# A Relu that writes back to its PSUM bank, in the index scores of a hybrid encoder trunk

## The chip, the cores and the metric

The kernel runs on one core of a Trainium2 chip. The time is the device time of one execution in microseconds (us); a kernel's number is the median of its runs. One further execution was recorded by the hardware profiler; all rows shown are of that one.

## What is computed

Two layers of a trunk over 512 frames of width 1024. Each layer projects the normalised input, runs four groups of mixers, gates them and adds the output projection:

```python
for l in range(DEPTH):
    h = _rmsnorm(x, norm_g[l])
    p = _split(h @ w_in[l])
    o_a = _mla(...)          # latent attention
    o_b = _diff_attn(...)    # differential attention, two maps per head
    o_c = _dsa(p["c_q"], p["c_k"], p["c_v"], p["c_qidx"], p["c_kidx"], p["c_widx"], rel_bias, topk)
    o_d = _short_conv(...)
    x = x + concat(o_a * silu(a_gate), ..., o_d * silu(d_gate)) @ w_out[l]
return _rmsnorm(x, final_g)
```

The change lies in group C, sparse attention, where an indexer of 8 heads scores every key for every query and each query attends to its 128 best keys:

```python
score = relu(einsum('bqhd,bkd->bqhk', qi, kidx))
index = einsum('bqh,bqhk->bqk', wi, score) * idx_scale
index = where(_chunk_mask(qpos, kpos)[None], index, NEG)
_, sel = lax.top_k(index, topk)
```

## The kernel before

Queries are worked in four blocks of 128 (`qb`), keys up to the end of the query's block, so a tile has `W = (qb + 1) * 128` columns. Large products are made as three float32r matmuls of high and low parts (`mm3`, L128); the parts are split by ScalarE (L107, L116, L119) and by GpSimd (L102) or VectorE (L117, L120).

A layer is a sequence of slots. Each slot merges streams of work: a `pair` of attention units (`unit_a` twice, `unit_b` twice, `unit_c` twice, L733, L762, L833) with projections for later slots. `index_scores` (L571) stands in the slot of the first `unit_a`. For every head pair `h0` it fetches the projected indexer queries from DRAM (`fetch`, L348) and then, for `qb` = 1, 2, 3 and both heads, makes one matmul into a PSUM bank (L587), a Relu on ScalarE into an SBUF tile of the tag "prob" (L590), and on VectorE the product with the head's weight: L593 for the first head, L595 for the seven others, which adds to the accumulator `ia[qb]` in SBUF. These are 24 tiles in each layer: 8 of 256, 8 of 384 and 8 of 512 columns. Block 0 needs no scores, since all of its keys are kept.

When an `ia[qb]` is complete, GpSimd masks its last columns (L600), and `select` (L602) finds the 128 best by 16 rounds of MAX8 and MATCH_REPLACE8 on VectorE (L608, L609); L613 makes the additive mask that `unit_c` feeds to TensorE (L841).

PSUM has eight banks: `BANKS = {"proj": 3, "s": 2, "pt": 2, "o": 1}`. The tag "s" serves the scores and the logits of all attention units: a `unit_a` writes its logits there (L742), VectorE takes the minimum (L744), ScalarE the exponential (L492), both reading the bank, and the bank is then free. "pt" holds transposes (L414). The tag "prob" has seven SBUF tiles. `unit_b` already writes the exponential of its second map back to its bank (`p = s if m else prob()`, L778), and VectorE combines both maps from there (L784).

The order of instructions on each engine isn't the program's. The kernel is built with a planner (`auto_bufs=True`) that runs through the program with costs of its own, lets no more tiles of a tag live at once than the tag has, picks on each engine whatever is ready and due first, and then gives the tiles addresses: a bank that one tag has left can be another tag's next. A waiting instruction on the chip waits for the last reader of whatever tile had its bank before. Each engine works through its queue in order.

Of the kernel before, what the change touches and what calls it, by code (L numbers as in the profile page):

```python
# [65 lines left out]
def hybrid_trunk(ctx, tc, x_in, norm_g, w_in, qa_g, w_uq, kva_g, w_ukv, dlam, subg,  # L66
# [16 lines left out]
    def bank(tag):  # L83
        return ps.tile([P, 512], FT, name=f"ps_{tag}", tag=tag, bufs=BANKS[tag])
# [7 lines left out]
    def prob():  # L92
        return pp.tile([P, 512], FT, name="prob", tag="prob")
# [221 lines left out]
    def layer(l, hT, enter, after):  # L315
# [32 lines left out]
        def fetch(d, m0, b1=0, c0=0):  # L348

            s = big()  # L350
            for r in range(2):
                for t in range(2):
                    src = d[r * b1 + t, 32 * m0:32 * m0 + 64, c0:].rearrange("(m p) n -> p m n", m=2)
                    nc.sync.dma_start(f(s)[r * 64 + t * 32:r * 64 + t * 32 + 32, :, c0:], src)
            return s
# [215 lines left out]
        def index_scores():  # L571
            kst = A["kst"]
            widx = A["widx"]
            for qb in range(1, NT):
                ia[qb] = pi.tile([P, (qb + 1) * P], FT, name=f"ia{qb}")
            qi = [fetch(qis[0], 0, c0=P)]
            yield 0.0
            for h0 in range(0, 8, 2):
                if h0 < 6:
                    qi.append(fetch(qis[(h0 + 2) // 4], (h0 + 2) % 4, c0=P))  # L580
                for qb in range(1, NT):
                    W = (qb + 1) * P
                    a = ia[qb]
                    for m in range(2):
                        h = h0 + m
                        s = bank("s")
                        nc.tensor.matmul(s[:, :W], lhsT=qi[h0 // 2][:, m, qb * P:(qb + 1) * P], rhs=kst[:, :W],  # L587
                                         start=True, stop=True)
                        r = prob()
                        nc.scalar.activation(r[:, :W], s[:, :W], AF.Relu)  # L590
                        w = widx[:, qb, h:h + 1]
                        if h == 0:
                            nc.vector.tensor_scalar(out=a, in0=r[:, :W], scalar1=w, scalar2=None, op0=OP.mult)  # L593
                        else:
                            nc.vector.scalar_tensor_tensor(out=a, in0=r[:, :W], scalar=w, in1=a,  # L595
                                                           op0=OP.mult, op1=OP.add)
                        yield 0.08 * (qb + 1)
            for qb in range(1, NT):
                W = (qb + 1) * P
                nc.gpsimd.memset(ia[qb][0:64, W - 64:W], -BIG)  # L600
# [361 lines left out]
        def once(what):  # L962
            if l == 0:
                what()
            yield 0.0

        work = {"qi": (10.4, index_proj), "is": (5.0, index_scores), "bl": (0.1, lambda: once(load_bias)), "bi": (0.1, lambda: once(build_bias)),
                "tb": (10.4, lambda: values("b", BV)), "tc": (10.4, lambda: values("c", CVC))}
        for a in range(2):
# [147 lines left out]
```

## Time and profile before

| | us |
|---|---|
| median of 3 runs | 655.87 (654.0 to 655.89) |
| the profiled execution | 653.91 |
| its span, first to last instruction | 652.1 |
| TensorE busy | 611.9 (94%) |
| VectorE busy | 501.6 (77%) |
| ScalarE busy | 376.0 (58%) |
| GpSimd busy | 259.1 (40%) |

PE is TensorE's matmuls and PEld its weight loads, DVE is VectorE, ACT ScalarE, POOL GpSimd. A busy share is a mean over stages with different limits; what the engines wait for in one stage is read from a window on that stage. PEclk is the TensorE clock that was granted, as a share of full speed. Matmul ends are modelled and matmuls overlap, so a busy TensorE is not one at its peak.

### The profile page before, as it was taken

What the parts mean: (1) busy time and instruction counts of PE and PEld (TensorE: products, weight loads), DVE (VectorE), ACT (ScalarE), POOL (GpSimd) and SP (SyncE); (2) the same over time, 40 slices, a digit from 0 to 9 for tenths busy, and PEclk for the clock granted to TensorE, in tenths of its full rate; (3) what the DMA queues carried; (4) which work ended last, traced back from release to release, by engine and by line L of the source; (5) the groups of instructions that cost most, each with busy time, mean ns of one, the idle gap of its engine ahead of it and who ended that gap; (6) DMA issues with size and microseconds to landing.
All of it is one profiled execution on the core that took longest, in us unless ns stands there. A gap on an engine that the chain in (4) does not pass through costs nothing. (4 is left out here: it accounts for less than half of the span.)

```text
span 652.1 us, 10775 instructions
## 1 busy us (share of the span) xinstructions
PE 611.9 (94%) x3461; PEld 515.9 (79%) x3467; DVE 501.6 (77%) x1496; ACT 376.0 (58%) x890; POOL 259.1 (40%) x368
## 2 busy tenths in 40 slices
PE   6989998899999999999989999999999999999995
PEld 4767876688788777799968787777878877779994
DVE  6776747999999987455494877799999998755537
ACT  5557556774653564665464567777566356556533
POOL 2275441233443353442441763234343535344340
PEclk9999997999999999999999999999999999999999
DMA  7447476843453611333252755573336551123203
GB/s 260 103 110 232 111 144 170 224 104 81 117 154 92 169 49 50 108 126 94 90 170 71 218 148 141 153 182 77 84 98 176 129 154 50 49 80 127 94 1 130
DMA packets 86555, 80.19 MB, mean 123 GB/s; under 512 B 7287, under 2 KB 73385, under 8 KB 86498
## 3 DMA queue, kind: packets, MB, share of 16 engines
q1 hardware_dynamic: 86498, 79.50, 43.9%
q8 instruction: 27, 0.44, 0.3%
q14 instruction: 30, 0.25, 0.1%
HBM read 64.70 MB, written 12.16 MB: 118 GB/s over the span
## 5 line engine op out<-in xcount | busy, mean ns | idle before, releaser
L102 POOL TENSOR_TENSOR wl<-wr,wh 128x256 fp32r<-128x256 f32 (+1 forms) x304 | 224.5, 771 | 310.8 <-ACT wh L107 217.9
L128 PE MATMUL ps_proj<-big,wh 128*128 128x512 f32 x768 | 251.8, 401 | 1.9 <-DVE big L117 1.0
L128 PE MATMUL ps_proj<-wh,big 128*128 128x256 f32 (+2 forms) x768 | 170.0, 307 | 4.2 <-DVE big L117 3.1
L128 PEld LDWEIGHTS ps_proj<-big,wh 128*128 128x128 f32 x768 | 140.4, 190 | 26.1 <-DVE big L117 1.7
L128 PE MATMUL ps_proj<-big,wl 128*128 128x512 f32 x384 | 152.4, 397 | 0.0
L128 PEld LDWEIGHTS ps_proj<-wh,big 128*128 128x128 f32 x768 | 128.4, 192 | 9.3 <-DVE big L117 2.3
L128 PE MATMUL ps_proj<-wl,big 128*128 128x256 f32 (+2 forms) x384 | 116.5, 303 | 0.0
L107 ACT CAST wh<-wr 128x1024 fp32r<-128x1024 f32 (+2 forms) x84 | 84.0, 1002 | 46.3 <-PE ps_proj L128 28.8
L128 PEld LDWEIGHTS ps_proj<-big,wl 128*128 128x128 f32 x384 | 72.4, 189 | 14.1
L128 PEld LDWEIGHTS ps_proj<-wl,big 128*128 128x128 f32 x384 | 74.0, 193 | 2.3 <-POOL wl L102 0.3
L116 ACT CAST pth<-ps_pt 128x128 fp32r<-128x128 f32 (+1 forms) x96 | 41.0, 427 | 40.6 <-PE ps_pt L414 40.3
L117 DVE TENSOR_TENSOR ptl<-ps_pt,pth 128x128 fp32r<-128x128 f32 (+1 forms) x96 | 46.7, 486 | 17.8 <-ACT pth L116 16.6
L492 ACT ACTIVATE prob<-ps_s,st_a 128x128 f32<-128x128 f32 (+1 forms) x64 | 33.8, 529 | 38.9 <-DVE st_a L744 19.8
L414 PE MATMUL ps_pt<-ident,prob 128*128 128x128 f32 x240 | 44.9, 285 | 11.7 <-ACT prob L496 5.3
L414 PEld LDWEIGHTS ps_pt<-ident,prob 128*128 128x128 f32 x240 | 28.0, 141 | 31.8 <-ACT prob L496 14.9
L609 DVE MATCH_REPLACE8 ia<-m,ia 128x256 f32<-128x256 f32 (+2 forms) x96 | 52.0, 545 | 0.2
L608 DVE MAX8 m<-ia 128x8 f32<-128x256 f32 (+2 forms) x96 | 50.9, 551 | 0.1
L496 ACT ACTIVATE prob<-prob,st_a 128x128 f32<-128x128 f32 (+1 forms) x64 | 36.1, 565 | 12.9 <-DVE st_a L495 12.8
L102 POOL TENSOR_TENSOR big<-prob,big 128x256 fp32r<-128x256 f32 x32 | 23.8, 767 | 35.9 <-ACT big L405 35.9
L452 PE MATMUL ps_o<-pth,vt 128*128 128x256 f32 (+1 forms) x144 | 35.2, 269 | 2.1 <-DVE prob L482 0.9
L452 PE MATMUL ps_o<-ptl,vt 128*128 128x256 f32 (+1 forms) x144 | 34.0, 283 | 0.0
L595 DVE SCALAR_TENSOR_TENSOR ia<-prob,widx,ia 128x256 f32<-128x256 f32 (+2 forms) x42 | 28.4, 690 | 6.3 <-ACT prob L590 5.1
(162 smaller groups left out, 963.9 us busy)
## 6 DMA issues: line engine op xcount, KB each, us to landing
wr<-in_w_in_dram SPq DMA_DIRECT2D x56, 512.0 KB
big<-trip SPq DMA_DIRECT2D x64, 128.0 KB
trip<-big SPq DMA_DIRECT2D x28, 256.0 KB
big<-in_x_dram SPq DMA_DIRECT2D x7, 512.0 KB
wr<-in_w_in_dram SPq DMA_DIRECT2D x8, 416.0 KB
big<-trip SPq DMA_DIRECT2D x32, 96.0 KB
wr<-in_w_out_dram SPq DMA_DIRECT2D x8, 384.0 KB
big<-big SPq DMA_DIRECT2D x8, 256.0 KB
```

The lines of the kernel that those rows point to most:

```text
L102: nc.gpsimd.tensor_tensor(out=o[:, c], in0=a[:, c], in1=b[:, c], op=OP.subtract)
L107: nc.scalar.copy(h[:, :n], raw[:, :n])
L116: nc.scalar.copy(hi, src)
L117: nc.vector.tensor_tensor(out=lo, in0=src, in1=f(hi), op=OP.subtract)
L128: nc.tensor.matmul(o, lhsT=a, rhs=b, start=start and i == 0 and j == 0, stop=stop and i == n - 1 and j == 2, skip_group_check=skip)
L414: i = nc.tensor.transpose(b[:, k * P:(k + 1) * P], p[:, k * P:(k + 1) * P], ident)
L452: i = nc.tensor.matmul(o[:, 256 * j + c:256 * j + 256], lhsT=v[:, kb, j * P:(j + 1) * P], rhs=x[:, kb, c:256], start=n == 1, stop=n == 2 * nb,
L492: nc.scalar.activation(p[:, :W], s[:, :W], AF.Exp, scale=-1.0, bias=mn, accum_out=sums)
L496: nc.scalar.activation(p[:, :W], p[:, :W], AF.Copy, scale=st[:, 2:3])
L595: nc.vector.scalar_tensor_tensor(out=a, in0=r[:, :W], scalar=w, in1=a, op0=OP.mult, op1=OP.add)
L608: nc.vector.max(out=m8, in_=a)
L609: nc.vector.match_replace(out=a, in_to_replace=m8, in_values=a, imm_value=MARK)
```

## The change

The Relu of a score tile writes into the PSUM bank that the matmul filled, over its own input; the weighted sum (L593, L595) reads it there. No "prob" tile is taken for it.

```diff
                         s = bank("s")
                         nc.tensor.matmul(s[:, :W], lhsT=qi[h0 // 2][:, m, qb * P:(qb + 1) * P], rhs=kst[:, :W],
                                          start=True, stop=True)
-                        r = prob()
+                        r = s
                         nc.scalar.activation(r[:, :W], s[:, :W], AF.Relu)
                         w = widx[:, qb, h:h + 1]
                         if h == 0:
```

## Rows read from the trace of the kernel before

**Rows 1.** The page: busy us (share of span, instructions), and VectorE in 40 slices.

```profile
PE 611.9 (94%) x3461; PEld 515.9 (79%) x3467; DVE 501.6 (77%) x1496; ACT 376.0 (58%) x890; POOL 259.1 (40%) x368
...
DVE  6776747999999987455494877799999998755537
```

**Rows 2.** Busy time by stretch: length, PE, PEld, DVE, ACT, POOL, granted clock, DMA.

```profile
90.00:100.00 10.00, 7.95 (x38) 6.08 (x37) 4.05 (x6) 4.67 (x9) 6.29 (x8) 0.99 0.79 186
100.00:110.00 10.00, 8.61 (x32) 7.03 (x33) 6.76 (x15) 6.05 (x14) 0.00 (x0) 0.67 0.76 186
110.00:120.00 10.00, 7.75 (x43) 6.27 (x42) 9.64 (x22) 7.85 (x18) 2.04 (x6) 1.00 0.57 164
400.00:430.00 30.00, 28.22 (x142) 22.85 (x140) 23.35 (x46) 22.67 (x55) 8.98 (x13) 1.00 0.45 138
```

**Rows 3.** Timeline of TensorE: start, us, instruction, count, idle before it and releaser.

```profile
97.74 0.40 PE L587 MATMUL ps_s<-kst,big 128*128 128x512 f32 x1
100.46 0.79 PE L587 MATMUL ps_s<-kst,big 128*128 128x256 f32 x2 [2.32 <-DVE ptl L117]
102.18 0.79 PE L128 MATMUL ps_proj<-big,wh 128*128 128x512 f32 x1 [0.93 <-DVE big L120]
```

**Rows 4.** Timeline of VectorE in the same stretch (the first row is two widths, two each).

```profile
96.43 3.64 DVE L595 SCALAR_TENSOR_TENSOR ia<-prob,widx,ia 128x256 f32<-128x256 f32 x4 [1.38 <-ACT prob L590]
99.99 0.41 DVE L117 TENSOR_TENSOR ptl<-ps_pt,pth 128x256 fp32r<-128x256 f32 x1
...
100.79 0.74 DVE L595 SCALAR_TENSOR_TENSOR ia<-prob,widx,ia 128x512 f32<-128x512 f32 x1
101.45 0.68 DVE L120 SCALAR_TENSOR_TENSOR big<-ps_proj,big 128x512 fp32r<-128x512 f32 x1
```

**Rows 5.** Busy time by stretch, as in rows 2, in slices of 1 us.

```profile
99.00:100.00 1.00, 0.00 (x0) 0.00 (x0) 0.90 (x3) 0.00 (x0) 0.66 (x1) 0.92 0.69 262
100.00:101.00 1.00, 0.54 (x2) 0.50 (x2) 1.00 (x4) 0.04 (x1) 0.00 (x0) 0.50 0.00 0
107.00:108.00 1.00, 1.00 (x6) 0.81 (x5) 0.16 (x1) 0.98 (x3) 0.00 (x0) 1.00 1.18 205
```

**Rows 6.** Groups by line and shape: count, busy us, mean ns, idle before.

```profile
L492 ACT ACTIVATE prob<-ps_s,st_b 128x512 f32<-128x512 f32 x8 | 5.5, 691 | 6.3 <-DVE st_b L504 4.5 <-DVE st_b L782 1.8
L492 ACT ACTIVATE ps_s<-ps_s,st_b 128x512 f32<-128x512 f32 x8 | 5.3, 656 | 1.4 <-DVE st_b L504 1.4
...
L595 DVE SCALAR_TENSOR_TENSOR ia<-prob,widx,ia 128x256 f32<-128x256 f32 (+2 forms) x42 | 28.4, 690 | 6.3 <-ACT prob L590 5.1
...
L784 DVE SCALAR_TENSOR_TENSOR prob<-ps_s,st_b,prob 128x256 f32<-128x256 f32 x8 | 3.8, 474 | 0.0
L784 DVE SCALAR_TENSOR_TENSOR prob<-ps_s,st_b,prob 128x384 f32<-128x384 f32 x8 | 4.9, 612 | 0.0
L784 DVE SCALAR_TENSOR_TENSOR prob<-ps_s,st_b,prob 128x512 f32<-128x512 f32 x8 | 5.9, 742 | 0.0
...
L744 DVE TENSOR_REDUCE st_a<-ps_s 128x1 f32<-128x512 f32 x8 | 5.5, 681 | 0.0
L593 DVE TENSOR_SCALAR ia<-prob,widx 128x512 f32<-128x512 f32 x2 | 1.9, 960 | 0.0
```

**Rows 7.** The chain of waits in layer 1: start, us, engine, tile, line.

```profile
402.46 0.86 DVE ia L593
...
404.24 0.96 DVE ia L593
```

**Rows 8.** Timeline of the burst's start; then what L590 and L587 waited for (us, times).

```profile
95.70 0.56 PE L587 MATMUL ps_s<-kst,big 128*128 128x384 f32 x2
96.02 1.41 ACT L590 ACTIVATE prob<-ps_s 128x256 f32<-128x256 f32 x4
...
  PE ps_s L587: 2.8, 5
...
  ACT prob L590: 0.5, 2
```

## The prediction

> **What bounds the kernel now.** I read the page's busy times and VectorE's slices first [rows 1]: TensorE is busy 611.9 of 652.1 us, VectorE 501.6, and VectorE has two long stretches at nine tenths. They follow the two places where the index scores are made, since the top-k search (L608, L609) lives on VectorE and can begin only when scores are complete. Then I cut out the score stages [rows 2]: in 90 to 110 us of layer 0 TensorE falls to 7.95 and 8.61 of 10 us and its granted clock to 0.67 in the second; from 110 us VectorE is at 9.64. In layer 1 (400 to 430 us) TensorE keeps 28.22 of 30 us and VectorE has 23.35. So in the stages that the change touches no engine is full the whole time, and behind them two nearly are. A gain or a loss there is worth what it does to TensorE's waits and to the start of the search.
>
> The one large hole is in layer 0. TensorE's last score matmul before it ends at 98.14 us; the next waits 2.32 us for VectorE's L117, and the projection after it 0.93 us for L120 [rows 3]. VectorE's own order [rows 4] says why: L117 stands behind four weighted sums (L595) that take 3.64 us together, and L120 behind a fifth. The idle time costs clock as well: the grant is 0.92 on average in the slice from 99 us, 0.50 from 100 us, and 1.00 again by 107 [rows 5]. 0.50 is the lower of the two levels, 1.2 GHz. From 102.2 to about 106.4 us TensorE works at it, 4.2 us for work that needs 2.1. The hole costs 3.25 + 2.1 = 5.4 us. The grant fell some 1.7 us after the last matmul ended.
>
> **The change part by part.** Nothing is taken from any queue: the same 48 matmuls, Relus and sums run, 24 in each layer, and no DMA moves. Three prices and one lifetime change.
>
> The Relu (L590) now writes PSUM. The same step stands in unit_b, whose exponential goes to an SBUF tile for one map and back to its bank for the other: 691 against 656 ns at 512 columns [rows 6]. 48 times 35 ns are at most 1.7 us of ScalarE, and ScalarE isn't full: 22.67 of 30 us in layer 1's stage [rows 2]. I take -0.2, with the ends 0 and -1.7.
>
> The weighted sum (L595) now has one operand in PSUM and one in SBUF. That form too is in the trace, L784: 474, 612 and 742 ns at 256, 384 and 512 columns. L595 has a mean of 690 over 42 in these three widths, 14 of each, where L784's prices would give 609 [rows 6]. The excess is in sums that run beside GpSimd's subtractions (L102), as those at 96.43 us do: four took 3.64 us; at the price of L784 they are 2 x 0.474 + 2 x 0.612 = 2.17, 1.47 us less [rows 4, 6]. All 42 fall from 28.4 to 25.6 us.
>
> The first product of each width (L593, six) is an instruction with one tensor operand. I price it by L744, which reads one PSUM operand: 681 ns at 512 columns against 960 now [rows 6], 0.28 less, and about as much for the next width, whose one in layer 1 took 0.86 [rows 7]. The Trainium skill speaks against this part: its page "VectorE: DVE Perf Modes", section "Mode 2×_2P — use both read ports for one tensor", says that PSUM has a single read port, so that a one-operand fp32 instruction loses there the doubled rate that it can have in SBUF. By that rule alone L593 gets slower and the sum below by some tenths larger; by the rows it gets faster, since 960 ns for 512 columns is no doubled rate. The trace decides for the rows.
>
> Now the path. In layer 0, with the order as it is, L117 comes 1.47 us earlier, the first wait shrinks from 2.32 to 0.85 us and ends before the clock falls: -1.5 - 2.1 = -3.6 us. But the order isn't fixed: the planner makes it anew from the new lifetimes. The ends are 0 and the whole hole, -5.4; I take the middle, -2.7, since neither row says which order comes. In layer 1 the chain of waits runs through L593 twice [rows 7]; at the price above these fall by about 0.28 each, 0.6 in all. Ends 0 and -0.6; I take -0.3, the middle.
>
> The lifetime: the bank was free when the Relu ended, and is now free when the weighted sum ends. TensorE takes its instructions in order, so a score matmul that waits for its bank holds up the projections (L128) and transposes (L414) queued behind it, and for those wait the splits on ScalarE and VectorE. The added time is at least the sum itself: 48 x 0.69 = 33 us [rows 6], 16.5 in each layer. In a burst it is more: the Relus of the four that started at 96.02 us were through at 97.43 [rows 8], their sums at 100.07 [rows 4]. With two tiles ("s": 2) 16.5 us stretch a stage by 8.2 us if the banks bind. What a stretch costs is what idles meanwhile on the engine that is full later: VectorE is idle 18% of 100 to 120 us and 22% of 400 to 430 [rows 2], so 1.5 + 1.8 = 3.3 us; with bursts half as much again, +5. The low end is 0: TensorE waited 0.5 us in the whole span for a Relu to free a bank, and the four Relus in a row from 96.02 us find four tiles filled, the last two by matmuls that began at 95.70 [rows 8], where the tag has two: the eight banks go round among all tags, and a free one is often at hand. I take +2.0, nearer the low end, because these rows are of the matmuls in question.
>
> Beside this stands the page "PSUM — Partial Sum Buffer" of the Trainium skill, section "Summary: rules for kernel authors": evacuate promptly, the space is tight. By that rule alone the banks bind and this part is at its +5; by the wait row it is 0. It is the second rival below.
>
> The freed "prob" tiles count for nothing: L590 waited for its matmul alone, 2.8 us in all [rows 8], never for a tile.
>
> The sum: -0.2 - 2.7 - 0.3 + 2.0 = -1.2 us. The profiled execution took 653.91 us (span 652.1), so 652.7 for one like it. It lies 1.96 us under the median of the runs, 655.87; on the median the sum gives 654.7.
>
> **The rivals.**
> *The hole closes (faster).* If the longer lifetime makes the planner spread the burst, L119 and L120 go ahead of the sums on their queues, and the next projection starts when its bank is free of them. Then 5.4 us come back whole, with layer 1's 0.6, and little is paid for banks: -6, so 650. For it: L784 has a sum's price without any lengthening, and in the ten microseconds with the burst VectorE was busy only 4.05 [rows 2]. Against it: an order in which the next tile waits for four sums instead of four Relus starts with the same burst.
> *The banks bind (slower).* In layer 1 a score matmul comes to wait for a sum that is queued on VectorE behind L117, L744 and a split. It decides from the point where TensorE stands for more than the 1.7 us after which the clock fell in layer 0: such a hole costs 5.4 us, as there, and without a gain in layer 0 that is 661. For it: sums lagged their Relus by 2.6 us in the burst, more than that point. Against it: the wait row of [rows 8].
> *Nothing reaches the path.* The savings fall into idle time, a spare bank is at hand, the burst stays: 655.9.
>
> **How the numbers follow.** 0.3% of 655.87 is 2.0 us, about what a measurement of this kernel can tell from no change. Gains and lifetime nearly cancel, 654.7, own range 652 to 657: 0.40, of which 0.27 within 0.3% and 0.13 faster. The hole closes, 650: 0.24, all faster. The banks bind, 661: 0.28, all slower. Nothing reaches the path: 0.08, of which 0.06 within and 0.02 slower. Together faster 0.37, within 0.33, slower 0.30. The range runs from 649 (the hole, layer 1's 0.6 and part of ScalarE's 1.7) to 663 (the second rival with part of the stretch, +2), which leaves out some 2 in 10.
>
> **What would show it.** Right: L595 at about 0.47, 0.61 and 0.74 us whether GpSimd works or not; L590 some 30 ns shorter; TensorE's idle time between 95 and 107 us under 2 us and the grant above 0.9 there. The lifetime's price shows as L587, or whatever takes the bank next, waiting for L595, and as a later first L608 in each layer. Wrong: sums as long as before; a new hole with a fallen clock in layer 1; or work far from the score stages moved so much by the planner that the difference arises there, which no term here counts.

## The result, and the profile after

| | before | after |
|---|---|---|
| median of 4 runs each, us | 654.93 (653.79 to 655.89) | 661.04 (659.74 to 662.92) |
| the profiled execution, us | 653.91 | 662.92 |
| its span, us | 652.1 | 661.2 |

The changed kernel takes 1.0086 of the time before, 95% interval 1.0065 to 1.0108: some 6 us slower, where 1.2 us less was forecast. One execution among those below, the profiled one of run e6, ran at a mean granted clock of 0.848 where every other had 0.97 or more; neither its time nor its profile is used. The page's busy times, to be read against [rows 1]:

```profile
PE 616.6 (93%) x3461; PEld 521.1 (79%) x3467; DVE 503.9 (76%) x1496; ACT 375.6 (57%) x890; POOL 258.6 (39%) x368
```

No work was added: TensorE has the same 3461 matmuls on record. They took 4.7 us more in all, and the span grew by 9.1. So part of the loss is matmuls at a lower clock, the rest is waiting, and the views by stretch must say where. The score stages first (length, PE, PEld, DVE, ACT, POOL, granted clock, DMA; the same stretches as [rows 2]), then TensorE's waits between 95 and 107 us, as in [rows 3], the first a group of two matmuls:

```profile
90.00:100.00 10.00, 8.86 (x42) 6.92 (x41) 2.93 (x6) 4.47 (x9) 5.62 (x8) 1.00 0.95 236
100.00:110.00 10.00, 8.88 (x45) 7.26 (x44) 7.24 (x15) 6.77 (x16) 0.00 (x0) 1.00 0.63 171
110.00:120.00 10.00, 9.75 (x54) 8.31 (x52) 8.75 (x19) 7.20 (x15) 4.36 (x8) 1.00 0.63 165
400.00:430.00 30.00, 29.80 (x150) 24.50 (x149) 21.23 (x44) 22.45 (x51) 8.46 (x12) 1.00 0.58 155
```

```profile
96.24 0.48 PE L587 MATMUL ps_s<-kst,big 128*128 128x256 f32 x2 [0.18 <-issue]
98.31 0.50 PE L128 MATMUL ps_proj<-big,wh 128*128 128x512 f32 x1 [0.96 <-DVE big L120]
```

The hole of 3.25 us in layer 0 has shrunk to 1.1 us and the grant stays at 1.00. Up to here the changed kernel is ahead: the 500th of TensorE's 3467 weight loads starts at 120.5 us instead of 124.0. Later it loses all of that and more. These are windows over layer 0, first of the kernel before, then of the changed one (same columns):

```profile
80.00:120.00 40.00, 33.31 (x154) 26.48 (x153) 26.69 (x55) 24.91 (x58) 11.58 (x18) 0.91 0.68 156
120.00:160.00 40.00, 38.75 (x246) 33.50 (x245) 39.32 (x125) 24.90 (x63) 13.88 (x20) 1.00 0.51 124
160.00:205.00 45.00, 43.88 (x259) 37.29 (x258) 43.19 (x147) 24.31 (x57) 15.60 (x23) 1.00 0.54 147
205.00:265.00 60.00, 57.47 (x292) 45.77 (x293) 50.42 (x191) 34.58 (x85) 27.12 (x38) 1.00 0.28 74
```

```profile
80.00:120.00 40.00, 37.25 (x186) 30.36 (x184) 25.21 (x54) 25.55 (x58) 13.43 (x21) 1.00 0.69 163
120.00:160.00 40.00, 36.36 (x234) 32.38 (x232) 37.21 (x116) 25.24 (x66) 11.60 (x18) 0.96 0.52 130
160.00:205.00 45.00, 44.23 (x261) 37.71 (x261) 44.10 (x153) 25.02 (x57) 18.34 (x27) 1.00 0.52 136
205.00:265.00 60.00, 52.42 (x249) 41.74 (x248) 50.98 (x177) 29.32 (x77) 23.31 (x31) 0.91 0.25 68
```

In 80 to 120 us TensorE is busy 3.9 us more. In 120 to 160 it is busy 2.4 less, and in 205 to 265, where the second `unit_b` runs beside the end of the search, 5.05 less, with the grant at 0.91. Where time is lost is read best from the starts of TensorE's weight loads, since all kernels make the same number of them. The changed kernel stands at +1.7 us at the 320th, -3.5 at the 500th, -3.0 at the 1000th (208.0 us instead of 211.0), +2.0 at the 1100th, +7.3 at the 1200th (258.4 instead of 251.1), +7.2 at the 1700th, +8.8 at the 1850th (365 us) and +9.0 at the last. So nearly all that is lost, 10.3 us, is lost between 208 and 258 us. The 1.6 between the 1700th and the 1850th are a fallen clock (last section), and the rest of layer 1 adds 0.2.

TensorE's two longest waits in 205 to 265 us, and what VectorE, then ScalarE did ahead of the first (changed kernel; start, us, instruction):

```profile
219.95 0.66 PE L414 MATMUL ps_pt<-ident,prob 128*128 128x128 f32 x2 [3.53 <-DVE prob L784]
...
252.19 0.39 PE L452 MATMUL ps_o<-ptl,vt 128*128 128x256 f32 x1 [1.82 <-DVE ptl L117]
```

```profile
215.95 1.01 DVE L608 MAX8 m<-ia 128x8 f32<-128x512 f32 x2
216.89 0.07 DVE L609 MATCH_VALUE_LOAD ia<-m,ia 128x8 f32 x1
216.95 0.67 DVE L609 MATCH_REPLACE8 ia<-m,ia 128x512 f32<-128x512 f32 x1
217.54 0.07 DVE L609 MATCH_VALUE_LOAD ia<-m,ia 128x8 f32 x1
217.61 0.40 DVE L609 MATCH_REPLACE8 ia<-m,ia 128x256 f32<-128x256 f32 x1
217.93 0.15 DVE L781 RECIPROCAL st_b<-st_b 128x1 f32<-128x1 f32 x1
218.00 0.54 DVE L608 MAX8 m<-ia 128x8 f32<-128x384 f32 x1
218.46 0.35 DVE L782 SCALAR_TENSOR_TENSOR st_b<-st_b,lamn,ep 128x1 f32<-128x1 f32 x1
218.74 0.68 DVE L608 MAX8 m<-ia 128x8 f32<-128x512 f32 x1
219.34 0.46 DVE L784 SCALAR_TENSOR_TENSOR prob<-ps_s,st_b,prob 128x256 f32<-128x256 f32 x1
```

```profile
216.27 1.04 ACT L107 CAST wh<-wr 128x1024 fp32r<-128x1024 f32 x1 [1.00 <-PE ps_proj L128]
217.22 0.44 ACT L492 ACTIVATE ps_s<-ps_s,st_b 128x256 f32<-128x256 f32 x1
217.59 0.19 ACT L492 ACTIVATION_READ_ACCUMULATOR ps_s<-ps_s,st_b 128x1 f32 x1
```

The grant falls at both waits (changed kernel, columns as above):

```profile
215.00:225.00 10.00, 6.47 (x24) 5.25 (x23) 9.79 (x39) 2.86 (x7) 2.77 (x4) 0.67 0.27 79
250.00:260.00 10.00, 8.18 (x39) 6.72 (x38) 6.46 (x24) 3.26 (x10) 1.12 (x2) 0.83 0.13 42
```

The two waits are 5.35 us, and the grants of 0.67 and 0.83 take 3.3 and 1.7 us more; together that is about the 10.3. TensorE's queue has no further projection ahead of the transpose L414, which waits for L784, and L784 stands behind steps of the search: of the 3.4 us from 215.95 us to its start 3.0 are L608 and L609. Not all of that is the search's doing. The exponential of the second map (L492), whose sum L781 needs, stands on ScalarE behind a weight cast (L107) of 1.04 us, and is through only at 217.78 us. From then on 1.1 us of steps lie before L784; how the rest divides between the cast and the steps ahead of 217.78 these rows don't say. Of the second wait no row shows that the search has to do with it: the last step started at 220.3 us.

The search is late. L609's share of VectorE, first before, then after (length, VectorE's busy us and instructions, two to a step; clock, DMA):

```profile
110.00:170.00 60.00, 16.02 (x54) 1.00 0.49 123
...
215.00:230.00 15.00, 1.34 (x4) 1.00 0.53 125
```

```profile
110.00:170.00 60.00, 13.01 (x44) 0.97 0.51 128
...
215.00:230.00 15.00, 2.88 (x9) 0.77 0.18 52
```

Five of the 48 steps of layer 0 have moved from the first stretch to later ones, though the first step starts at 116 us instead of 120. The last of the three masks (L600), after which the last block can be searched, came 4.7 us later. GpSimd's last L600 in layer 0, before and after:

```profile
116.90 0.14 POOL L600 MEMSET ia<- 64x64 f32 x1 [2.39 <-DVE ia L595]
```

```profile
121.63 0.14 POOL L600 MEMSET ia<- 64x64 f32 x1
```

Did score matmuls wait for their banks, as the second rival said? All that L587 waited for sums in the changed kernel, and the Relu for L587 (us in total, times, longest; the Relu's 10.7 were 2.8 before, [rows 8]):

```profile
ACT ps_s L590 <- PE ps_s L587: 10.7, 14, 2.4
...
PEld ps_s L587 <- DVE ia L595: 0.6, 2, 0.4
```

0.6 us, in weight loads, in the whole span. No bank was waited for on the chip to speak of. What changed is the order that the planner made from the lifetimes: from 80 to 85 us on (GpSimd's from 112) each engine's queue is another one.

### The profile page after: what moved, and what is told of

The parts are those of the page before. It is cut to its first block, busy times and chain, and to the rows that moved or that the text cites. A ratio compares the mean times of both kernels' runs of the same rounds, so it can differ in the third digit from the quotient of the medians.

```text
span 661.2 us, 10761 instructions
## 1 busy us (share of the span) xinstructions
PE 616.6 (93%) x3461; PEld 521.1 (79%) x3467; DVE 503.9 (76%) x1496; ACT 375.6 (57%) x890; POOL 258.6 (39%) x368
## 5 line engine op out<-in xcount | busy, mean ns | idle before, releaser
L128 PE MATMUL ps_proj<-big,wh 128*128 128x512 f32 x768 | 255.8, 405 | 2.7 <-DVE gate L398 1.1
L128 PEld LDWEIGHTS ps_proj<-big,wh 128*128 128x128 f32 x768 | 142.0, 192 | 28.1 <-DVE gate L398 1.3
L107 ACT CAST wh<-wr 128x1024 fp32r<-128x1024 f32 (+2 forms) x84 | 83.7, 998 | 43.1 <-PE ps_proj L128 22.6
L117 DVE TENSOR_TENSOR ptl<-ps_pt,pth 128x128 fp32r<-128x128 f32 (+1 forms) x96 | 46.2, 484 | 18.0 <-ACT pth L116 17.0
L414 PE MATMUL ps_pt<-ident,prob 128*128 128x128 f32 x240 | 44.0, 284 | 15.2 <-DVE prob L784 8.7
L492 ACT ACTIVATE prob<-ps_s,st_a 128x128 f32<-128x128 f32 (+1 forms) x64 | 33.7, 528 | 34.0 <-DVE st_a L504 15.5
L414 PEld LDWEIGHTS ps_pt<-ident,prob 128*128 128x128 f32 x240 | 27.9, 141 | 31.7 <-ACT prob L496 13.1
L609 DVE MATCH_REPLACE8 ia<-m,ia 128x256 f32<-128x256 f32 (+2 forms) x96 | 51.7, 541 | 0.1
L608 DVE MAX8 m<-ia 128x8 f32<-128x256 f32 (+2 forms) x96 | 50.8, 547 | 1.1 <-POOL ia L600 0.9
L452 PE MATMUL ps_o<-ptl,vt 128*128 128x256 f32 (+1 forms) x144 | 35.0, 290 | 1.9 <-DVE ptl L117 1.8
L452 PE MATMUL ps_o<-pth,vt 128*128 128x256 f32 (+1 forms) x144 | 36.0, 272 | 0.3 <-DVE prob L482 0.2
L595 DVE SCALAR_TENSOR_TENSOR ia<-ps_s,widx,ia 128x256 f32<-128x256 f32 (+2 forms) x42 | 25.7, 614 | 8.7 <-ACT ps_s L590 7.7
```

The source lines that it names most:

```text
L107: nc.scalar.copy(h[:, :n], raw[:, :n])
L117: nc.vector.tensor_tensor(out=lo, in0=src, in1=f(hi), op=OP.subtract)
L128: nc.tensor.matmul(o, lhsT=a, rhs=b, start=start and i == 0 and j == 0, stop=stop and i == n - 1 and j == 2, skip_group_check=skip)
L414: i = nc.tensor.transpose(b[:, k * P:(k + 1) * P], p[:, k * P:(k + 1) * P], ident)
L452: i = nc.tensor.matmul(o[:, 256 * j + c:256 * j + 256], lhsT=v[:, kb, j * P:(j + 1) * P], rhs=x[:, kb, c:256], start=n == 1, stop=n == 2 * nb,
L492: nc.scalar.activation(p[:, :W], s[:, :W], AF.Exp, scale=-1.0, bias=mn, accum_out=sums)
```

## The experiments

Five theories came up on the way; the expectations call some of them rivals. **A**: the loss is the chance of one order, and any small edit draws another. **B**: each layer pays for the longer life of its banks. **C**: the loss belongs to the new prices or lifetimes in whatever order. **D**: the longer life of the score tiles, with two to the tag, makes the planner place scores later; the search starts later and its last steps get in `unit_b`'s way. **E**: search steps are worth much in any order. All times are medians in us; ratios are to the kernel before, run beside them on the same chip, with 95% intervals. The last column is where layer 1's first score matmul starts in the profile (before 398.7, after 407.5).

| run | what | median | ratio | layer 1 |
|---|---|---|---|---|
| e1 | change in layer 0 alone | 660.58 | 1.0051 (1.0025 to 1.0077) | 406.6 |
| e2 | change in layer 1 alone | 655.60 | 1.0008 (0.9983 to 1.0034) | 400.9 |
| e3 | bank held, else as before | 657.39 | 1.0022 (0.9996 to 1.0047) | 400.6 |
| e4 | own tag, no prob tile | 654.95 | 0.9980 (0.9959 to 1.0001) | 399.9 |
| e14 | both lifetimes, old prices | 659.64 | 1.0046 (1.0023 to 1.0069) | 404.8 |
| e5, e6 | PW 10.5: after, before | 660.81, 658.36 | 1.0093 (1.0063 to 1.0123), 1.0050 (1.0025 to 1.0075) | 404.1, - |
| e7, e8 | "is" 6.0: after, before | 666.02, 659.13 | 1.0161 (1.0122 to 1.0199), 1.0065 (1.0041 to 1.0090) | 406.4, 405.3 |
| e15, e16 | PW 9.5: after, before | 661.43, 656.83 | 1.0055 (1.0035 to 1.0075), 0.9991 (0.9976 to 1.0006) | 401.8, 402.8 |
| e9, e10 | three tiles: after, before | 653.32, 649.38 | 0.9968 (0.9942 to 0.9993), 0.9913 (0.9886 to 0.9940) | 399.6, 399.0 |
| e18 | three tiles, PW 10.5, before | 657.48 | 1.0022 (0.9996 to 1.0049) | 406.2 |
| e11, e12 | 8 rounds: after, before | 650.89, 659.27 | 0.9921 (0.9891 to 0.9952), 1.0066 (1.0040 to 1.0092) | 395.6, 402.3 |
| e13, e17 | 14 rounds: after, before | 650.42, 660.20 | 0.9886 (0.9863 to 0.9909), 1.0080 (1.0052 to 1.0107) | 396.7, 400.9 |

**Which layer.** e1 and e2:

```diff
-                        r = s
+                        r = s if l == 0 else prob()
```

```diff
-                        r = s
+                        r = prob() if l == 0 else s
```

> The change in layer 0 alone; in layer 1 the Relu goes to an SBUF tile as before. The order of the instructions in layer 0 is that of the changed kernel. Theory A (the loss arises in layer 0 between 205 and 265 us, in unit_b and the search, from the new order of the instructions): 5 to 8 us over the kernel before, thus all of the loss, with TensorE as idle in 205 to 265 us as in the changed kernel. Rival B (each layer pays for its longer bank lifetime): about half, 3 us over the kernel before.

> The change in layer 1 alone; layer 0 is in the order of the kernel before. Theory A: within 1 us of the kernel before, since the changed layer 1 was as long as the old one. Rival B: about 3 us over it.

Layer 0 alone costs 0.51%, layer 1 alone nothing that can be told from zero. The 0.51% is 3.4 us, less than the 5 to 8 of A and near the 3 of B, but its interval overlaps that of the whole change, and the trace decides: the queues in e1 are those of the changed kernel all through layer 0, and so are the waits: 3.52 us before L414 at 218.89 us and 1.82 before L452 at 251.26, with 52.43 us busy in 205 to 265. That they came again in another execution shows that they belong to this order. Layer 1 has the same lifetimes and pays nothing, so B falls: the cost isn't one of each layer.

**Which lifetime.** e3 holds the bank to the sum's end and leaves the rest; e4 takes no prob tile and leaves the bank; e14 does both:

```diff
-                        w = widx[:, qb, h:h + 1]
+                        w = s[:, 0:1]
```

```diff
-                        r = prob()
+                        r = pp.tile([P, 512], FT, name="rel", tag="rel", bufs=2)
```

> The Relu goes to an SBUF tile as before, but the sum takes its scalar, which is the head's weight in the kernel before, from the first column of the score bank, so that the bank lives until the sum's end (the scores are therefore weighted by another number). The lifetime alone, with the prices of before. Theory B (bank lifetime costs): slower by 4 to 8 us as the changed kernel is, with score matmuls that wait for sums. Theory A (the new order costs, wherever it happens to fall): the order is neither that of before nor that of the changed kernel, the waits of score matmuls for sums stay under 2 us in all, and the time lies anywhere within 8 us of the kernel before on either side.

> The Relu goes to an SBUF tile of a tag of its own with two buffers; banks are freed at the Relu's end as before, and no prob tile is taken. No price and no bank lifetime changes, only the order. Theory A: the order alone moves the time by some us, so a difference of 2 us or more from the kernel before is likely, of either sign. Theory B: within 1 us of the kernel before, since the banks live as long as there.

> Both lifetimes of the change with the instructions of before: the Relu goes to an SBUF tile of a tag of its own with two buffers, no prob tile is taken, and the sum takes its scalar from the first column of the score bank, so that the bank lives until the sum ends (the scores are weighted by another number than the head's weight). If the lifetimes make the order that costs (Theory D): 657 to 663 us, the last mask of layer 0 at 119 us or later and more than 3 late search steps from 215 us on. If it is the chance of one order (Theory A): anything from 650 to 663 us, with masks and late steps that need not go together.

Held banks alone: 0.22%, which can't be told from zero, with 1.3 and 0.8 us of waits of L587 for sums (weight loads and matmuls) and 3.0 and 2.5 of L414, whose banks the scores had had before. Its last mask is late too, at 120.1 us, but only three search steps start after 215 us. Own tag alone: nothing, or a little less. B had expected 4 to 8 us of e3, and A some 2 us of e4, so both miss here. Together, with the instructions and prices of before, they cost 0.46%, and the profile has the same face as the changed kernel's: the last mask of layer 0 late, and late search steps. GpSimd's last L600 and L609 in 215 to 230 us, of e14:

```profile
122.54 0.14 POOL L600 MEMSET ia<- 64x64 f32 x1
```

```profile
215.00:230.00 15.00, 3.08 (x10) 0.77 0.26 68
```

TensorE's longest wait in 205 to 265 us is the first of the changed kernel's two over again; the second isn't there (e14):

```profile
221.34 0.66 PE L414 MATMUL ps_pt<-ident,prob 128*128 128x128 f32 x2 [3.52 <-DVE prob L784]
```

So the lifetimes alone, through the planner, give a slower order of this kind, with the same wait at the same place. Between the 1000th and the 1200th weight load they lose 6.3 of the 10.3 us. By ratio they give 3.0 us, against 3.4 of e1 and 5.6 of the whole change; whether the rest belongs to the prices or to the draw these runs don't say.

**Is it one order or many?** Two numbers that only weigh streams of the program against each other in a slot were changed in both kernels:

```diff
-PW = 10.0
+PW = 10.5
```

```diff
-"is": (5.0, index_scores)
+"is": (6.0, index_scores)
```

> The changed kernel with PW 10.5 instead of 10.0: the work that the merge ascribes to the attention units in a slot, which moves the order of the program slightly and nothing else. Theory A (the loss is that of one order): the time moves by 2 us or more, and falls back towards the kernel before, 653 to 659 us. Rival C (the loss belongs to the changed prices or lifetimes, in whatever order): 3 to 8 us over the kernel before, and as much over the next run, which has the same PW without the change.

> The kernel before with PW 10.5 instead of 10.0. Theory A: an order of its own again, within 2 us of the changed kernel at this PW or on either side of it. Rival C: 3 to 8 us faster than the changed kernel at this PW.

> The changed kernel with 6.0 instead of 5.0 as the work ascribed to the index scores in their slot: another slight move of the order. Theory A: 653 to 659 us. Rival C: 3 to 8 us over the next run.

> The kernel before with 6.0 instead of 5.0 as the work ascribed to the index scores. Theory A: within 2 us of the changed kernel with 6.0, or on either side of it. Rival C: 3 to 8 us faster than that.

> The changed kernel with PW 9.5 instead of 10.0. Theory D: later masks in layer 0 than in the next run, and 3 to 7 us slower than that. Theory A: on either side of the next run.

> The kernel before with PW 9.5. The measure for the run ahead of it; 652 to 660 us.

The kernel before, with nothing changed but a weight, takes 656.8 to 659.1 us, up to 0.65% more: an order by itself is worth some 4 us. But the changed kernel did not fall back to 653 to 659 in any of the three, as A wanted. It is slower than its partner by 2.5 (where the intervals overlap), 6.9 and 4.6 us, and with e9 and e10 (3.9) and the original pair that makes five of five. Against the pure chance of A this speaks for C or D. D's mark, the late mask, goes with it: 125 against 121 us at 6.0, 120 against 118 at PW 9.5.

The place doesn't go with it. At the 1200th weight load e7 is 0.3 us ahead of e8 and e15 1.1 ahead of e16; they fall behind, by 5.6 and 2.7 us in the profiles, only in layer 1, which was not followed up. So these two pairs repeat the sign and not the mechanism of the original pair, and what makes the sign the same in five pairs is not shown. Nor are the late search steps a mark of the change alone: e8, without the change, has 4.45 us of L609 in 215 to 230 us and TensorE at 53.26 us in 205 to 265, and is slow too.

What most of the profiles do share is the stretch in which the changed kernel loses its 10.3 us, from the 1000th to the 1200th weight load. Against the kernel before, the other kernels that hold the banks in layer 0 and search in full (e1, e3, e5, e7, e9, e14, e15) lose 10.5, 5.1, 1.9, 7.0, 5.6, 6.3 and 7.4 us there. Those that don't hold them (e2, e4, e8, e10, e16, e18) lose 0.0, 2.3, 7.1, 0.8, 1.6 and 1.8. e5 and e8 are the exceptions, and each number is of one execution.

**A third tile for the scores.**

```diff
-BANKS = {"proj": 3, "s": 2, "pt": 2, "o": 1}
+BANKS = {"proj": 3, "s": 3, "pt": 2, "o": 1}
```

> The changed kernel with three tiles of the tag s instead of two, so that the planner may start a third score while two wait for their sums. Theory D (the longer life of a score tile under the cap of two delays the scores; the search then starts later and gets in the way of unit_b, whose transposes wait for L784): the last mask of layer 0 comes back from 122 to about 117 us, the wait of L414 in 205 to 265 us goes, 653 to 657 us. Theory A (chance of one order): anything from 653 to 664 us, whatever the time of the masks.

> The kernel before with three tiles of the tag s. Theory D: no lack of score tiles there, so within 2 us of the kernel before. Theory A: an order of its own, anything from 653 to 664 us.

> The kernel before with three tiles of the tag s and PW 10.5. If score tiles are what the planner is short of, it is 4 to 9 us under the same PW with two tiles (658.6 us), so 649 to 655 us; if the gain at PW 10.0 was the luck of one order, 654 to 661 us.

With three tiles the changed kernel is 7.7 us faster than with two (medians 653.32 and 661.04), and its last mask is back (GpSimd's last L600 in layer 0, and L609 in 215 to 230 us, of e9):

```profile
116.06 0.14 POOL L600 MEMSET ia<- 64x64 f32 x1
```

```profile
215.00:230.00 15.00, 1.24 (x3) 0.89 0.13 41
```

That is as D said, and the long wait of L414 is gone. But TensorE still waits 1.12 us for L784 and 1.71 for L117 there, and e9 loses the 5.6 us above. What D didn't say either: the kernel before gains 0.87%, 5.7 us, too. Its layer 1 starts when it did, but there the eighth search step (L609) comes at 437 instead of 447 us and the last at 523 instead of 530. With 649.38 us it is the fastest version with the whole search and beats both kernels, and the change makes it slower. At PW 10.5 the third tile brings 0.9 us (657.48 against 658.36), which the intervals don't tell from nothing. So it isn't a gain in every order.

**Are the late search steps what costs?** e11 to e13 and e17 leave out rounds of the search:

```diff
-            for rnd in range(16):
+            for rnd in range(14):
```

> The changed kernel with 8 instead of 16 rounds of the search (it keeps the 64 best keys instead of 128), some 40 us less work on VectorE in all. Theory D: the search no longer fills VectorE, so the changed kernel is within 2 us of the next run or faster. Rival C (prices or lifetimes cost by themselves): still 4 to 7 us slower than the next run.

> The kernel before with 8 instead of 16 rounds of the search (64 best keys). It is only the measure for the run ahead of it; by itself it says how much of the time hangs on the search: if VectorE bounds the stretches of the search, some 20 to 40 us less than the kernel before, if TensorE does, under 10.

> The changed kernel with 14 instead of 16 rounds of the search (112 best keys): the last six MAX8 and MATCH_REPLACE8 steps of each layer fall away, some 6 us of VectorE's work. Theory D (late steps of the search in 205 to 230 us hold up unit_b): TensorE's hole near 220 us before L414 goes and layer 1 begins by about 400 us instead of 407, as with 8 rounds; 652 to 657 us. Theory A (the search is not the place, the order with 8 rounds was another draw): 658 to 663 us.

> The kernel before with 14 rounds of the search (112 best keys), the control for the changed kernel with 14. Theory D (late search steps hold up unit_b in the changed kernel; the kernel before has two such steps from 215 us on): it gains 4 us or less, 652 to 657 us, so the changed kernel with 14 rounds (650.4 us) is the faster of the two. Rival E (six steps are worth ten microseconds in any order): 645 to 648 us.

e13 is the sharpest run. By line and tile its queues are those of the changed kernel up to 211 us on VectorE and 212 on TensorE; then the last six steps of the search in layer 0 are gone. In 205 to 265 us, and L609 alone from 215 us:

```profile
205.00:265.00 60.00, 57.25 (x291) 44.81 (x290) 48.75 (x181) 32.61 (x82) 24.68 (x34) 1.00 0.29 80
```

```profile
215.00:230.00 15.00, 0.00 (x0) 1.00 0.18 52
```

TensorE is at 57.25 instead of 52.42 us, the grant at 1.00, and no wait in 205 to 265 us is longer than 0.6 us. The 1000th weight load starts 0.5 us earlier than in the changed kernel, the 1100th 4.8 and the 1200th 9.4: of the 10.3 us that the changed kernel loses in this stretch, e13 loses 1.5. So the loss goes with the late steps. It need not all be their own time, for from 211 us on the order is another one too: in e13 the cast (L107) stands behind the exponential (L492) and not ahead of it. In all e13 is 10.6 us faster than the changed kernel by medians on different chips, 2.0% or 13 us by the ratios. That is more than D's 652 to 657, since a layer 1 in another order gains some as well. The kernel before has two steps after 215 us; without its last six it gains nothing and loses 0.8%, which was in nobody's numbers and can only be its order: E falls. With 8 rounds it is the same. The changed kernel is faster than its partner by 8.4 us at 8 rounds and by 9.8 at 14 (on different chips; ratio of the ratios 0.981), and slower in all five pairs with 16. At the 1200th weight load it is 5.1 and 4.2 us ahead of them: there what the change gains in the score stage is kept, with no search steps after 215 us. The remainder arises in layer 1.

What stays open: why the planner, with longer lives, places scores late, is argued from the masks and the third tile and not shown in the planner itself; where the second wait comes from, and why the changed kernel falls behind in layer 1 in two other orders, no run says; and the two shorter searches' controls show that an edit of this size moves a kernel by 4 to 5 us through its order alone, so no single pair weighs much.

## Why the prediction was wrong

*The weighted sum (right).* Forecast 0.47, 0.61 and 0.74 us whether GpSimd works or not, 25.6 us together; the rows say 481, 614 and 746 ns and 25.7. *The Relu (nearly).* 383, 494 and 599 ns became 362, 478 and 583, so 16 to 21 instead of 35. Groups by line and shape of the changed kernel, to be read against [rows 6]:

```profile
L595 DVE SCALAR_TENSOR_TENSOR ia<-ps_s,widx,ia 128x512 f32<-128x512 f32 x14 | 10.4, 746 | 3.0 <-ACT ps_s L590 2.8
L595 DVE SCALAR_TENSOR_TENSOR ia<-ps_s,widx,ia 128x384 f32<-128x384 f32 x14 | 8.6, 614 | 2.0 <-ACT ps_s L590 1.8
L595 DVE SCALAR_TENSOR_TENSOR ia<-ps_s,widx,ia 128x256 f32<-128x256 f32 x14 | 6.7, 481 | 3.8 <-ACT ps_s L590 3.1
```

*The first product (right sign, wrong reason).* L593 at 512 columns fell from 960 to 750 ns, not to 681. But the kernel before has it in three widths, and the smallest turns the argument round. L593, first before, then after:

```profile
L593 DVE TENSOR_SCALAR ia<-prob,widx 128x384 f32<-128x384 f32 x2 | 1.7, 848 | 0.4 <-ACT prob L590 0.4
L593 DVE TENSOR_SCALAR ia<-prob,widx 128x256 f32<-128x256 f32 x2 | 0.7, 354 | 3.0 <-ACT prob L590 3.0
```

```profile
L593 DVE TENSOR_SCALAR ia<-ps_s,widx 128x512 f32<-128x512 f32 x2 | 1.5, 750 | 0.1
L593 DVE TENSOR_SCALAR ia<-ps_s,widx 128x384 f32<-128x384 f32 x2 | 1.2, 618 | 0.4 <-ACT ps_s L590 0.4
L593 DVE TENSOR_SCALAR ia<-ps_s,widx 128x256 f32<-128x256 f32 x2 | 1.0, 484 | 3.0 <-ACT ps_s L590 3.0
```

At 256 columns, where GpSimd is idle, it got slower, 354 to 484 ns. That agrees with the Trainium skill, "VectorE: DVE Perf Modes", section "Mode 2×_2P — use both read ports for one tensor", which the prediction set aside on the row of 960 ns. During that instruction GpSimd's subtractions ran for 679 of the 960 ns, so the row couldn't show that the mode is lacking.

*The hole of layer 0 (right, too small).* Taken at half, -2.7; it closed. From the 320th weight load to the 500th the changed kernel won 5.2 us (+1.7 to -3.5), about the whole 5.4, and to the 1000th 4.7. Rival one, "the hole closes", is what happened up to 208 us.

*Layer 1's chain (can't be told):* e2 stands at 1.0008 (0.9983 to 1.0034), and -0.3 us is less than the runs can tell.

*The life of the banks (this step failed).* +2.0, with 0 and +5 as ends, was worked out as waits on the chip and as idle time of VectorE inside the score stages. The waits came out as 0.6 us. (The 0.5 us of waits before, from which the low end was read, are those of L587 alone; the transposes L414 waited another 0.9 us for Relus.) The price was paid elsewhere: the planner has two tiles with longer lives to plan with, the last mask comes 4.7 us later, the search with it, and its tail stands ahead of the second `unit_b`'s work, 100 us after the scores. From the 1000th to the 1200th weight load the changed kernel loses 10.3 us, against the 2.0 of the sum, and twice its upper end; e13, without the late steps, loses 1.5, and e14, with the lifetimes alone, 6.3. The step of the argument that failed is "what a stretch costs is what idles meanwhile on the engine that is full later": the engine that was full later, VectorE, did not lack time (50.98 us busy in 205 to 265 against 50.42) but had the wrong thing at the head of its queue, and TensorE stood. The text named this at its end, work far from the score stages, as what no term counts.

*The freed prob tiles (right as far as can be told):* e4 lies between 0.9959 and 1.0001. Together with the held bank they may weigh more (e14 against e3), which the prediction left out.

*The rivals.* "The banks bind" gave 661, which is the time measured, by a mechanism that did not occur: in layer 1, on the chip, by a score matmul that waits. In layer 1 nothing was lost to such waits. That the range held the time was luck: the reason was not in it. Nor is the 1.7 us a point at which a clock falls: a wait of 1.84 us left the grant at 1.00 (last section). The page "PSUM — Partial Sum Buffer" of the Trainium skill, section "Summary: rules for kernel authors" (evacuate promptly, the space is tight) had the sign right. The trace doesn't show banks that bind on the chip, with 0.6 us of waits; what has its sign is a third score tile for the planner to plan with, which gave 7.7 us with the change and 5.7 without, though 0.9 in another order.

## What to carry to other kernels

In a kernel whose order is planned, a longer life of a tile is a new order for the whole program: price it not only by waits for that tile but by what the work that follows on it does to the stages behind, above all a long serial job like a search that has to end by a certain time. A gain in TensorE's stage can be kept or eaten 100 us later, so read milestones along the span and not the stage alone. And a small difference of two planned kernels says little before both have been built in some neutral variants: here an order alone was worth 4 to 5 us, and the change 2.5 to 6.9 us in five pairs with the whole search, but -8.4 and -9.8 with a shorter one.

## What the runs showed of the hardware that was not expected

**The one-operand product is cheaper from SBUF alone, and dearer beside GpSimd.** L593 in SBUF took 354 ns at 256 columns with GpSimd idle, and 848 and 960 at 384 and 512 with its subtractions running over most of each. From PSUM it took 484, 618 and 750, though GpSimd ran beside the 618 too. The sum L595, with two operands, gains nothing from SBUF: with GpSimd idle it took about 0.48, 0.61 and 0.75 us before as after, and only its ten of 42 beside the subtractions were longer, 0.76 to 1.08 us. The price of an instruction on VectorE with SBUF operands is therefore to be read from rows with the same neighbour.

**The same wait costs the clock in one execution and not in another.** TensorE waited 1.84 us for L635 at about 43 us in both kernels, before the queues of any engine differ. A second place is a wait of 2.02 us for L117 in layer 1, at 335 us before and 342 after. The stretches behind both, before and then after:

```profile
40.00:50.00 10.00, 8.15 (x43) 6.57 (x41) 8.55 (x18) 4.45 (x7) 9.85 (x14) 1.00 0.78 219
338.00:343.00 5.00, 5.00 (x30) 4.42 (x29) 4.78 (x14) 3.23 (x9) 1.77 (x2) 1.00 0.69 210
```

```profile
40.00:50.00 10.00, 8.16 (x32) 6.23 (x31) 7.59 (x17) 3.12 (x6) 9.34 (x13) 0.83 0.75 203
345.00:350.00 5.00, 5.00 (x23) 4.36 (x22) 3.42 (x12) 3.37 (x9) 0.56 (x1) 0.68 0.66 202
```

The grant stayed at 1.00 before and fell to 0.83 and 0.68 after; each time the changed kernel lost about 1.6 us. It isn't the change: of the 19 profiles read here the grant fell at the first place in three (e10, the kernel before with three tiles, is one) and at the second in 15. So 3.3 of the 9.1 us between the two profiled spans are two such falls, and the medians, 6.1 us apart, are the better measure of the change.
